# Moving one rotation step, the last outputs and the GELUs in the order of a hybrid layer on one core

## The chip, the core and the metric

The kernel runs on 1 core of one Trainium2 chip. Its time is the device time in microseconds (us) of that core, lower is better.

## The reference

One decoder layer over 256 tokens of width 2048, all in float32:

```python
h = rmsnorm(x)
q, k, v, u = split(h @ w_in, [1024, 1280, 1536])
a = sliding_window_attention(rmsnorm(q), rmsnorm(k), v)   # 16 heads of 64, 4 kv heads, window 128, bias, sinks
s = s5_mixer(u)                                           # 64 groups of 16 channels, 64 complex states
s = gelu(s + d * u); s = s * sigmoid(s @ w_glu)
x = x + concat(rmsnorm(a), rmsnorm(s)) @ w_out
x = x + (silu(rmsnorm(x) @ w_gate) * (rmsnorm(x) @ w_up)) @ w_down
```

## The kernel before

The weights stream from memory in pieces of 512 KB (`w`, 128 partitions x 1024 numbers, four buffers, issued by SyncE). Each piece is split in two: ScalarE's cast makes `whi` (`_piece`, L462) and VectorE's subtraction makes the rest, `wlo` (L463); each has two buffers. A piece feeds 12 matmuls of 128x512 on TensorE (L513 to L515: `whi`, `wlo` and `whi` again, against the high or the low part of the activations). In this order come 16 pieces of `w_u`, 24 of `w_qkv` (the last column block of keys and values first, then the two of queries, of 8 pieces each), 8 of `w_glu`, 32 of `w_out`, and those of the feed-forward part. "Piece 33" below is the 34th from the start.

The S5 mixer runs beside the `w_qkv` pieces, in four parts q=0 to 3 of 16 channel groups. A part has matrices (`m`, two halves, L229), tokens (`u`, L279), a rotation (`r`, L213), states (`s`, L296) and outputs (`o`, L339):

- `rotations` works out cosines `cs` and sines `sn` of a part: VectorE L221 to L223, ScalarE L224 to L226.
- `states` multiplies on TensorE (`px`), transposes into `pa` and `pb` (L310, L315), turns with the rotation on VectorE (`zz` L322, `hh` L323, sum L324), scans (L329) and turns back (L333 to L335).
- `outputs` makes `py` on TensorE (L347, L351); ScalarE copies it to `za` (L353) and issues the DMA write `zd<-za` (L354) to memory.
- `za` and `zz` have the same tag and one buffer between them; so `zz` of one part waits until the write of the part before has read `za`.
- For the matrices, GpSimd issues loads `kd<-kt` (L272) and eight loads `mt<-kd` (L276).

Behind it GpSimd reads `zd` back into `sm` (L692), ScalarE applies the GELU (L695), TensorE transposes into `pt_z` (L697), ScalarE and VectorE split that into `zT` (L698) and `wT` (L699), the operands of the `w_glu` matmuls.

The norms of keys and queries come per token tile (0 and 1), for the keys (4 heads) and then the queries (16 heads): ScalarE squares (`sq`, L713), VectorE sums (`sh`, L715) and scales (L716), GpSimd takes the power -1/2 (`rqk`, L717), VectorE scales the queries' factors (`rqk`, L718) and multiplies the keys (`kvn`, L721). TensorE transposes the keys into `pt_k` (L725). Attention runs in four quads of heads: `pt_q` (L738), `qT` on ScalarE (L739), logits `pl0` and `pl1` on TensorE (L744, L748), `lg` on VectorE (L756) and the exps on ScalarE (L764, L768). The glu has its sigmoids on ScalarE (`sg`, L805 and L808), and L563 there splits what `w_out` multiplies.

What sets the order: each engine's instructions are put in order before the run, by the priority at which a part of the program is traced and by a model of when the inputs are ready; at run time an engine keeps that order and waits. The mixer's steps are all traced at one priority, in the order of the string `STEPS`. `tc.issue_after(mark)` keeps outputs(q) behind the cast of piece `PY_AT[q]`, and the GELU of part q behind that of piece `GELU_AT[q]`:

```python
else:
    with tc.issue_after(marks[PY_AT[q]][1]):
        ssm.outputs(q)
```

Of the kernel before, what the change touches and what calls it, by code (L numbers as in the profile page):

```python
# [39 lines left out]
WORK = dict(tag="t", bufs=4)  # L40


STEPS = "m0a m0b r0 u0 m1a u1 s0 m1b r1 o0 u2 m2a s1 u3 m2b r2 o1 m3a s2 m3b r3 o2 s3 o3"

U_AT = (0, 0, 18, 19)
PY_AT = (14, 19, 25, 32)
GELU_AT = (34, 35, 36, 37)

HEADS = [0, 4, 1, 5, 2, 6, 3, 7, 8, 12, 9, 13, 10, 14, 11, 15]

# [417 lines left out]
def layer_kernel(ctx: ExitStack, tc: tile.TileContext, ins, out):  # L468
# [11 lines left out]
    @contextmanager  # L480
    def prio(at):

        was, tc.cur_priority = tc.cur_priority, at
        try:
            yield
        finally:
            tc.cur_priority = was
# [173 lines left out]
    with prio(20_000):  # L661
        for step in STEPS.split():
            q = int(step[1])
# [8 lines left out]
# [3 lines that stand above are left out]
# [12 lines left out]
    with prio(55_000):  # L687
        for q in range(ngc):
            cols = slice(q * GC * GP, (q + 1) * GC * GP)
            pt = ps.tile([P, 2, L], F32, name="pt_z", **WORK)  # L690
            for t in range(NT):
                nc.gpsimd.dma_start(sm[t][:, cols].rearrange("p (b x) -> p b x", x=UB),  # L692
                                    ssm.zd[4 * q : 4 * q + 4, t * P : (t + 1) * P].rearrange("b p x -> p b x"))
                with tc.issue_after(marks[GELU_AT[q]][0]):
                    s.activation(sm[t][:, cols], sm[t][:, cols], AF.Gelu_apprx_tanh)  # L695
# [268 lines left out]
```

## Time and profile before

| | |
|---|---|
| median of 3 runs | 1066.85 us (1066.33 to 1067.28) |
| profiled execution | 1064.85 us, its span 1063.1 us |
| TensorE (PE) busy | 1043.2 us, 98% |
| VectorE (DVE) busy | 610.9 us, 57% |
| ScalarE (ACT) busy | 485.4 us, 46% |
| GpSimd (POOL) busy | 56.1 us, 5% |

Times in a trace count from the start of the span. An engine is idle either for want of an input, which then has a releaser, or because its order makes it stand behind an instruction that waits. A matmul's row starts when it enters TensorE; the next one may start before it ends, so that the distance between starts counts. `L463` is line 463 of the kernel.

### The profile page before, as it was taken

What the parts mean: (1) busy time and instruction counts of PE and PEld (TensorE: products, weight loads), DVE (VectorE), ACT (ScalarE), POOL (GpSimd) and SP (SyncE); (2) the same over time, 40 slices, a digit from 0 to 9 for tenths busy, and PEclk for the clock granted to TensorE, in tenths of its full rate; (3) what the DMA queues carried; (4) which work ended last, traced back from release to release, by engine and by line L of the source; (5) the groups of instructions that cost most, each with busy time, mean ns of one, the idle gap of its engine ahead of it and who ended that gap; (6) DMA issues with size and microseconds to landing.
All of it is one profiled execution on the core that took longest, in us unless ns stands there. A gap on an engine that the chain in (4) does not pass through costs nothing.

```text
span 1063.1 us, 13209 instructions
## 1 busy us (share of the span) xinstructions
PE 1043.2 (98%) x5048; PEld 820.8 (77%) x5048; DVE 610.9 (57%) x755; ACT 485.4 (46%) x665; POOL 56.1 (5%) x87
## 2 busy tenths in 40 slices
PE   7999988999999999999999999999999999999998
PEld 3457776767788888888888888888888888888886
DVE  6988975788556454445554455545555444444443
ACT  5244556665445444444444444444444333333332
POOL 2030325000000000000000000000000000000000
PEclk9999999999999999999999999999999999999999
DMA  7677567434455556555555555555655556565653
GB/s 268 191 197 237 152 180 267 165 109 139 158 189 167 182 193 189 189 183 194 189 189 195 180 197 185 193 191 184 198 181 196 179 190 207 195 201 195 203 192 101
DMA packets 62015, 199.08 MB, mean 187 GB/s; under 512 B 11328, under 2 KB 14000, under 8 KB 61632
## 3 DMA queue, kind: packets, MB, share of 16 engines
q1 hardware_dynamic: 52800, 184.89, 53.3%
q0 software_dynamic: 3264, 9.29, 3.3%
q10 hardware_dynamic: 5888, 4.06, 1.3%
q8 instruction: 39, 0.64, 0.3%
q14 instruction: 24, 0.20, 0.1%
HBM read 193.47 MB, written 4.74 MB: 186 GB/s over the span
## 4 chain that ended last, share of the span: by engine, by line
PE 85%; DVE 8%; ACT 2%; DMA 2%; issue 2%; POOL 1%; SPq 0%; DVEq 0%; POOLq 0%; ACTq 0%
PE acc L514 26%; PE acc L515 26%; PE acc L513 26%; PE acc L530 2%; DVE wlo L463 1%; PE pt_f L872 1%; DMA zd<-za 1%; POOL rqk L717 1%; PE po L786 1%; DVE bm L249 1%; ACT whi L462 1%; DVE cm L242 1%; DVE bm L250 1%; DVE tm L249 1%; DVE cm L243 1%
## 5 line engine op out<-in xcount | busy, mean ns | idle before, releaser
L463 DVE TENSOR_TENSOR wlo<-w,whi 128x1024 fp32r<-128x1024 f32 x328 | 401.7, 1225 | 407.4 <-ACT whi L462 407.1
L462 ACT CAST whi<-w 128x1024 fp32r<-128x1024 f32 x328 | 345.1, 1052 | 473.1 <-PE acc L515 461.4
L513 PE MATMUL acc<-whi,pTh 128*128 128x512 f32 x704 | 275.0, 391 | 0.0
L514 PE MATMUL acc<-wlo,pTh 128*128 128x512 f32 x704 | 274.0, 389 | 0.2 <-DVE wlo L463 0.2
L515 PE MATMUL acc<-whi,pTl 128*128 128x512 f32 x704 | 274.1, 390 | 0.1
L515 PEld LDWEIGHTS acc<-whi,pTl 128*128 128x128 f32 x704 | 132.1, 188 | 28.0 <-DVE pTl L564 0.5
L514 PEld LDWEIGHTS acc<-wlo,pTh 128*128 128x128 f32 x704 | 132.2, 188 | 27.6 <-DVE wlo L463 0.7
L513 PEld LDWEIGHTS acc<-whi,pTh 128*128 128x128 f32 x704 | 132.2, 188 | 27.6 <-ACT pTh L563 0.5
L513 PE MATMUL acc<-whi,fhi 128*128 128x512 f32 x352 | 139.0, 395 | 0.0
L514 PE MATMUL acc<-wlo,fhi 128*128 128x512 f32 x352 | 138.9, 395 | 0.0
L515 PE MATMUL acc<-whi,flo 128*128 128x512 f32 x352 | 138.9, 394 | 0.0
L515 PEld LDWEIGHTS acc<-whi,flo 128*128 128x128 f32 x352 | 66.3, 188 | 15.5
L513 PEld LDWEIGHTS acc<-whi,fhi 128*128 128x128 f32 x352 | 66.3, 188 | 15.5
L514 PEld LDWEIGHTS acc<-wlo,fhi 128*128 128x128 f32 x352 | 66.3, 188 | 15.3
L513 PE MATMUL acc<-whi,mT 128*128 128x512 f32 x128 | 50.9, 397 | 0.8 <-ACT mT L563 0.8
L514 PE MATMUL acc<-wlo,mT 128*128 128x512 f32 x128 | 50.5, 394 | 0.0
L515 PE MATMUL acc<-whi,nT 128*128 128x512 f32 x128 | 50.3, 394 | 0.0
L514 PE MATMUL acc<-wlo,hT 128*128 128x512 f32 x96 | 38.6, 402 | 2.8 <-DVE wlo L463 2.8
L515 PE MATMUL acc<-whi,lT 128*128 128x512 f32 x96 | 38.0, 396 | 0.0
L513 PE MATMUL acc<-whi,hT 128*128 128x512 f32 x96 | 37.7, 398 | 0.0
L530 PE MATMUL acc<-w,sm 128*128 128x512 f32 x64 | 30.7, 628 | 6.7 <-DVE sm L601 6.7
L884 ACT ACTIVATE sl<-acc,r 128x256 f32<-128x256 f32 x44 | 20.8, 472 | 20.7 <-PE acc L515 20.7
(258 smaller groups left out, 822.0 us busy)
## 6 DMA issues: line engine op xcount, KB each, us to landing
w<-in_w_gu SPq DMA_DIRECT2D x176, 512.0 KB, 3.3
w<-in_w_down SPq DMA_DIRECT2D x88, 512.0 KB, 3.4
w<-in_w_out SPq DMA_DIRECT2D x32, 512.0 KB, 3.3
w<-in_w_qkv SPq DMA_DIRECT2D x24, 512.0 KB, 4.3
w<-in_w_u SPq DMA_DIRECT2D x16, 512.0 KB, 4.0
w<-in_w_glu SPq DMA_DIRECT2D x8, 512.0 KB, 4.3
bias<-td POOLq DMA_DIRECT2D x4, 512.0 KB, 5.1
x<-in_x POOLq DMA_DIRECT2D x2, 1024.0 KB, 10.4
```

Of the source, the lines that this page charges most:

```text
L242: v.tensor_tensor(dst, bc(c[:, i, hs], 2, T), bc(e, 3, GP), op=ALU.mult)
L243: v.tensor_tensor(cmh[:, :, 1:], cmh[:, :, 1:], tm, op=ALU.subtract)
L249: v.tensor_tensor(dst, bc(b[:, i, hs], 2, T), bc(e, 3, GP), op=ALU.mult)
L250: v.tensor_tensor(bm2, bm2, tm2, op=ALU.add)
L462: self.marks.append([nc.scalar.copy(hi, w).ins])
L463: nc.vector.tensor_tensor(lo, w, hi.bitcast(F32), op=ALU.subtract)
L513: mm = pe.matmul(acc[t], lhsT=xh, rhs=whi, start=first, stop=False)
L514: pe.matmul(acc[t], lhsT=xh, rhs=wlo, start=False, stop=False)
L515: pe.matmul(acc[t], lhsT=xl, rhs=whi, start=False, stop=last)
L530: mm = pe.matmul(acc[t], lhsT=x(k)[:, t * P : (t + 1) * P], rhs=w, start=k == 0, stop=k == nk - 1)
L717: nc.gpsimd.tensor_tensor(r_[:, o : o + n], part, cst["mhalf"][:, :n], op=ALU.pow)
L884: s.activation(sl, acc[t][:, :256], AF.Silu, scale=r2[:, t : t + 1])
```

## The change

The rotation of part 3 (`r3`) is traced before the states of part 2 instead of behind `m3b`; the outputs of part 3 are kept behind the cast of piece 29 instead of 32; and each of the four GELUs behind that of one piece earlier. No instruction is added or removed.

```diff
--- before.py
+++ after.py
@@ -40,11 +40,11 @@
 WORK = dict(tag="t", bufs=4)
 
 
-STEPS = "m0a m0b r0 u0 m1a u1 s0 m1b r1 o0 u2 m2a s1 u3 m2b r2 o1 m3a s2 m3b r3 o2 s3 o3"
+STEPS = "m0a m0b r0 u0 m1a u1 s0 m1b r1 o0 u2 m2a s1 u3 m2b r2 o1 m3a r3 s2 m3b o2 s3 o3"
 
 U_AT = (0, 0, 18, 19)
-PY_AT = (14, 19, 25, 32)
-GELU_AT = (34, 35, 36, 37)
+PY_AT = (14, 19, 25, 29)
+GELU_AT = (33, 34, 35, 36)
 
 HEADS = [0, 4, 1, 5, 2, 6, 3, 7, 8, 12, 9, 13, 10, 14, 11, 15]
```

GpSimd's and SyncE's orders stay as they were, and TensorE's does from the second quad's logits on. Elsewhere on TensorE: part 3's output matmuls `py` stood in piece 37 and now stand in piece 38; and 336 weight matmuls of the stretch that starts with `w_qkv` stand before the first quad's `pl0` in place of 324, while 408 stand before the second quad's in both.

**VectorE, the states of part 3.** `hh` and `zz` are those of part 3, `wlo_721` belongs to piece 33 and `wlo_739` to piece 34. Before:

```order
L323 TENSOR_TENSOR hh_1540<-pb_1527,sn_1464 128x512
L463 TENSOR_TENSOR wlo_721<-w_718,whi_720 128x1024
L322 TENSOR_TENSOR zz_1539<-pa_1526,cs_1463 128x512
L327 MEMSET d0_1544 128x16
L324 TENSOR_TENSOR zz_1539<-hh_1540,zz_1539 128x512
L329 SCALAR_TENSOR_TENSOR gg_1547<-d0_1544,zz_1539 128x512
L463 TENSOR_TENSOR wlo_739<-w_736,whi_738 128x1024
```

Now:

```order
L323 TENSOR_TENSOR hh_1540<-pb_1527,sn_1370 128x512
L322 TENSOR_TENSOR zz_1539<-pa_1526,cs_1369 128x512
L463 TENSOR_TENSOR wlo_721<-w_718,whi_720 128x1024
L324 TENSOR_TENSOR zz_1539<-hh_1540,zz_1539 128x512
L329 SCALAR_TENSOR_TENSOR gg_1547<-d0_1544,zz_1539 128x512
L463 TENSOR_TENSOR wlo_739<-w_736,whi_738 128x1024
```

`wlo_721` stood between `hh` and `zz`; now it stands behind both.

**VectorE, the norms of keys and queries.** The digit in `sh0`, `rqk1` and `kvn1` is the token tile; 128x4 is for the keys, 128x16 for the queries. Before:

```order
L716 TENSOR_SCALAR sh0_1651<-sh0_1651 128x16
L716 TENSOR_SCALAR sh1_1665<-sh1_1665 128x4
L463 TENSOR_TENSOR wlo_1774<-w_1771,whi_1773 128x1024
L715 TENSOR_REDUCE sh1_1665<-sq_1672 128x16
L718 TENSOR_SCALAR rqk0_1652<-rqk0_1652 128x16
L721 TENSOR_TENSOR kvn1_78<-kvn1_78,rqk1_1666 128x256
L716 TENSOR_SCALAR sh1_1665<-sh1_1665 128x16
L463 TENSOR_TENSOR wlo_1792<-w_1789,whi_1791 128x1024
L718 TENSOR_SCALAR rqk1_1666<-rqk1_1666 128x16
```

Now:

```order
L716 TENSOR_SCALAR sh0_1651<-sh0_1651 128x16
L715 TENSOR_REDUCE sh1_1665<-sq_1667 128x4
L715 TENSOR_REDUCE sh1_1665<-sq_1672 128x16
L463 TENSOR_TENSOR wlo_1792<-w_1789,whi_1791 128x1024
L716 TENSOR_SCALAR sh1_1665<-sh1_1665 128x4
L716 TENSOR_SCALAR sh1_1665<-sh1_1665 128x16
L718 TENSOR_SCALAR rqk0_1652<-rqk0_1652 128x16
L718 TENSOR_SCALAR rqk1_1666<-rqk1_1666 128x16
L721 TENSOR_TENSOR kvn1_78<-kvn1_78,rqk1_1666 128x256
L463 TENSOR_TENSOR wlo_1916<-w_1913,whi_1915 128x1024
```

`kvn1` (L721) stood ahead of `rqk1` (L718) and now stands behind it, and one weight subtract is gone from between the norm's steps (it stands further ahead now). ScalarE's squares are now all behind part 3's two GELUs, of which one square stood ahead.

**ScalarE, where the first quad's exps begin** (`sg` is the glu's, `es` and `lg,dn` are exps of the first quad's logits, `whi` is a weight piece's cast). Before:

```order
L805 ACTIVATE sg<-acc_1733 128x512
L764 ACT_TABLE_LOAD
L764 ACTIVATE es<-es 128x8
L462 CAST whi<-w 128x1024
L808 ACTIVATE sg,sss<-sm_79 128x512
L768 ACTIVATE lg,dn<-lg,mx 128x128
L462 CAST whi<-w 128x1024
```

Now:

```order
L805 ACTIVATE sg<-acc_1733 128x512
L462 CAST whi<-w 128x1024
L808 ACTIVATE sg,sss<-sm_79 128x512
L764 ACT_TABLE_LOAD
L764 ACTIVATE es<-es 128x8
L462 CAST whi<-w 128x1024
L805 ACTIVATE sg<-acc_1734 128x512
L768 ACTIVATE lg,dn<-lg,mx 128x128 x2
L462 CAST whi<-w 128x1024
```

The table load and `es` stood ahead of the first L808 and now stand behind it. From that L808 to the second quad's `qT` there are eight exps, three L805, three further L808 and four L563 in both orders, but five casts where there were four.

## Rows read from the trace of the kernel before

**Rows 1.** The page's first part, and windows: window, TensorE's length and busy time first.

```profile
PE 1043.2 (98%) x5048; PEld 820.8 (77%) x5048; DVE 610.9 (57%) x755; ACT 485.4 (46%) x665; POOL 56.1 (5%) x87
...
185.10:216.00 30.90, 28.89 (x126) 21.05 (x126) 23.99 (x46) 20.61 (x45) 3.29 (x3) 1.00 0.53 176
216.00:330.00 114.00, 113.85 (x554) 87.47 (x554) 78.68 (x124) 66.42 (x143) 1.51 (x2) 1.00 0.44 143
```

**Rows 2.** Waits of TensorE in 140 to 216: total us, times, longest.

```profile
PE acc L514 <- DVE wlo L463: 2.9, 3, 2.2
PE pt_k L725 <- DVE kvn L721: 1.4, 1, 1.4
```

**Rows 3.** The chain in 138 to 216: start us, us, what.

```profile
141.96 6.12 DMA zd<-za
...
163.70 3.17 DMA zd<-za
...
168.14 3.93 DMA sm<-zd
```

**Rows 4.** Timeline of VectorE (DVE) around 146: start us, us, instruction, idle time before.

```profile
144.60 0.69 DVE L323 TENSOR_TENSOR hh<-pb,sn 128x512 f32<-128x512 f32 x1 [4.05 <-PE pb L315]
...
148.10 0.69 DVE L322 TENSOR_TENSOR zz<-pa,cs 128x512 f32<-128x512 f32 x1 [1.68 <-DMA zd<-za]
```

**Rows 5.** DMA issues in 78 to 82, then in 114 to 118: KB, us to landing.

```profile
zd<-za ACTq DMA_DIRECT2D x1, 256.0 KB, 7.8
...
zd<-za ACTq DMA_DIRECT2D x1, 256.0 KB, 4.8
```

**Rows 6.** Timeline of GpSimd (POOL), 115 to 187.

```profile
115.24 3.40 POOL L276 DMA_DIRECT2D mt<-kd  x7
...
138.35 3.86 POOL L276 DMA_DIRECT2D mt<-kd  x8 [3.15 <-PE acc L515]
...
172.89 1.04 POOL L717 TENSOR_TENSOR rqk<-sh,mhalf 128x4 f32<-128x4 f32 x1 [1.08 <-DVE sh L716]
...
178.52 3.92 POOL L717 TENSOR_TENSOR rqk<-sh,mhalf 128x16 f32<-128x16 f32 x2 [3.49 <-DVE sh L716]
183.06 3.81 POOL L717 TENSOR_TENSOR rqk<-sh,mhalf 128x16 f32<-128x16 f32 x1 [0.62 <-DVE sh L716]
```

**Rows 7.** Timeline of TensorE (PE), 154 to 211.

```profile
154.60 0.39 PE L513 MATMUL acc<-whi,hT 128*128 128x512 f32 x1
...
157.35 0.39 PE L513 MATMUL acc<-whi,hT 128*128 128x512 f32 x1
...
161.06 0.42 PE L347 MATMUL py<-mt,ua 128*32 128x128 f32 x8
...
182.95 0.55 PE L725 MATMUL pt_k<-pack,kvn 128*128 128x128 f32 x3 [1.37 <-DVE kvn L721]
...
210.65 1.02 PE L744 MATMUL pl<-kT,qT 128*128 128x256 f32 x4
```

**Rows 8.** Timeline of VectorE in 178 to 187.

```profile
178.63 1.23 DVE L463 TENSOR_TENSOR wlo<-w,whi 128x1024 fp32r<-128x1024 f32 x1
...
182.47 0.42 DVE L721 TENSOR_TENSOR kvn<-kvn,rqk 128x256 f32<-128x256 f32 x1 [0.81 <-POOL rqk L717]
...
182.89 1.22 DVE L463 TENSOR_TENSOR wlo<-w,whi 128x1024 fp32r<-128x1024 f32 x1
186.90 0.17 DVE L718 TENSOR_SCALAR rqk<-rqk 128x16 f32<-128x16 f32 x1 [2.79 <-POOL rqk L717]
```

**Rows 9.** Timeline of ScalarE (ACT), 194 to 210.

```profile
194.57 1.28 ACT L764 ACT_TABLE_LOAD   x1
...
195.98 1.03 ACT L462 CAST whi<-w 128x1024 fp32r<-128x1024 f32 x1
196.92 0.63 ACT L808 ACTIVATE sg<-sm 128x512 f32<-128x512 f32 x1
...
209.70 0.67 ACT L739 ACTIVATE qT<-pt_q,pack 128x512 f32<-128x512 f32 x1
```

## The prediction, before the changed kernel was run

> **What bounds the kernel now.** The page's first line gives TensorE 1043.2 us busy, 98% of the span [rows 1], so the kernel is a stream of matmuls and only TensorE's idle time can be won or lost. The windows say where that idle time lies: 0.15 us in 216 to 330, but 2.01 us in 185.1 to 216 alone [rows 1], and more ahead of it. The change reorders work before 216 alone (behind the second attention quad's first `pl0` the TensorE order is the same), so what counts is how late TensorE arrives there: 210.65 now [rows 7]. The waits view names what it waits for in this stretch: `wlo` from VectorE (2.9 us in all, once 2.2) and `pt_k` for `kvn` (1.4) first [rows 2]. The chain view goes one step further back. The 2.2 us wait ends a chain that comes through the DMA write `zd<-za` of 6.12 us; another, which ends in the GELUs and the `pt_z` transposes of q=3, goes through a write of 3.17 us and the read back `sm<-zd` of 3.93 us [rows 3]. The write is in VectorE's way because `zz` (L322) reuses the buffer `za` that the write reads: `zz` starts at 148.10, 1.68 us idle, released by that DMA [rows 4]. Everything counts against the profiled execution's 1064.85 us, 2.00 below the median of the runs; I add my difference to the median, 1066.85.
>
> **Part 1, the last states step.** No instruction is added or removed; 12 matmuls of a weight piece take 157.35 - 154.60 = 2.75 us [rows 7] on either side. Now `pa` and `pb` of q=3's states come earlier relative to what they need, which saves some 0.4 us: an estimate, from `hh` waiting until 144.60 for `pb` [rows 4]. In exchange the VectorE order puts both `hh` and `zz` ahead of the weight subtract `wlo_721`, where before only `hh` was. That subtract (1.23 us by another of its kind, [rows 8]) now waits for the write of q=2's output. I put its issue at 142.05, as before within 0.1 (the chain shows 141.96). How long it takes is not known. The four writes of this kernel took 3.2 to 7.8 us: 7.8 and 4.8 the first two [rows 5], 6.1 and 3.2 the last two [rows 3]. The 6.1 us write started behind all eight `mt` loads of its step (issued 138.35 to 142.21); the 4.8 us one at 115.69 went beside them (115.24 on) [rows 5, 6]. In the new order the `mt` loads are issued about 3 us later, alongside, which is nearest to 4.8. So the write lands at 146.85; `zz` at 146.9 takes 0.69; `wlo_721` runs 147.5 to 148.7, and TensorE waits some 2.1 us in that piece. The wait of 2.2 us one piece later then shrinks to about 0.4, as its subtract `wlo_739`, behind the same `zz` either way, ends 0.2 us sooner at about 151.7. Net at the next piece (154.60 before, [rows 7]): **-0.2 us**. One wait is swapped for another.
>
> **Part 2, the last outputs.** The diff queues them three pieces sooner, yet the TensorE order shows q=3's `py` one piece later (with its inputs due earlier, other work went ahead of it). Hence its start moves from 161.06 [rows 7] by 2.75 - 0.2 = 2.55 to 163.6, and with the same write, read back and GELU behind it (3.17 and 3.93 us, [rows 3]) the last GELU goes from 172.1 (168.14 + 3.93) to about 174.65.
>
> **Part 3, the k/q norm.** It is traced behind that GELU and now also runs behind it: ScalarE does both GELUs of q=3 before the first square, which was in front. GpSimd's 128x16 `pow` of token tile 0 started at 178.52 [rows 6], 6.4 us behind the last GELU. In the new order ScalarE has a cast and a copy `qn` less in between and a square more (-1.3, an estimate), VectorE one weight subtract more (+0.85, the part of its 1.23 that isn't beside ScalarE's work). So it starts 5.95 behind 174.65, at 180.6. On VectorE the new order then has `L718 rqk1` in front of `L721 kvn1`, which was the other way round. L718 needs the last 128x16 `pow`; TensorE's `pt_k` needs L721. Before, L721 waited only for the 128x4 `pow` (0.81 us, [rows 8]), and the last `pow`, 183.06 to 186.87, was beside the path, holding L718 at 186.90 [rows 6, 8]. Now it is on the path. What is one 128x16 `pow`? The pair of 3.92 us is one of 128x16 and one of 128x4; the latter alone took 1.04 us at 172.89 [rows 6], so 2.9. The single one took 3.81. The 2.9 one began before a weight subtract, the 3.81 one inside one (182.89 to 184.11, [rows 8]). In the new order none runs when the last `pow` starts, as VectorE stands at L718; I take 2.9, with 3.81 as bound (+0.9). Then: 180.6 + 2.9 + 1.04 = 184.55, + 2.9 = 187.45 for the last `pow`, about 0.6 us for L718, L721 and the hand-over (0.48 for the latter two, 182.47 to 182.95, [rows 7, 8]): `pt_k` at 188.1, where it was 182.95 [rows 7], 5.15 us later. TensorE has by then done 12 matmuls more (its order puts them ahead), 2.75 us. So the delay is **+2.4 us**, the -0.2 of part 1 included; the wait at `pt_k` grows from 1.4 to about 3.5 us.
>
> The Trainium skill's page "SBUF — State Buffer", section "Who interferes with whom", has a rule that speaks against the subtracts near these `pow`s: a VectorE instruction with two SBUF inputs and a GpSimd instruction that reads SBUF exclude each other, and the one that starts second waits for all of the first. The 3.81 us row agrees (it began 0.17 us into a subtract and took 0.9 more), but the other speaks against it: the subtract at 178.63, 0.11 us into a `pow`, took 1.23 us as ever [rows 8]. By the rule the time would be that of rival 4, by that row the forecast stands.
>
> **Part 4, ScalarE before the second quad.** Here the first quad's exps, the glu work and the casts fill ScalarE: 20.61 of 30.9 us in 185.1 to 216 [rows 1]. `qT` (L739) is ready at 209.70 + 0.67 and the second `pl0` follows at 210.65 [rows 7, 9], so ScalarE's order sets it. Between the first L808, at 196.92, and `qT` the new order has one cast more (1.03 us), and the exps' table load with `es` (194.57 to 195.98, 1.4 us), which stood ahead of that L808 [rows 9]: together 2.4 us. L808 itself I put 1.8 later rather than 2.4, since the table load is no longer ahead of it. So `qT` and the second `pl0` are 1.8 + 2.4 = 4.2 later, which is **+1.8** on top of the 2.4. TensorE, with 72 matmuls between the two `pl0` where 84 were, then waits about 2.5 to 3 us there. Of the 2.01 us idle some 0.4 lies behind it, in waits for the logits, and shrinks (an estimate): **-0.4 us**. Nothing else changes after 216, and no slack is left there to take it back (0.15 us, [rows 1]). The moved GELU at each earlier q costs nothing: its due time moves by one piece, and its input is there long before.
>
> **The sum**: 2.4 + 1.8 - 0.4 = **+3.8 us**, so 1068.65 for the profiled execution and 1066.85 + 3.8 = 1070.65, **1070.6**, for the median. Bounds: the write at 3.2 us gives -1.6, at 6.1 +1.3, at 7.8 +3.0; the `pow` at 3.81 gives +0.9. The forecast's own range is about 1069.1 to 1072.
>
> **Rivals.**
> 1. Not slower: ScalarE absorbs it. TensorE idles 2.01 us between 185.1 and 216 [rows 1]. If the table load and the added cast are through before TensorE gets to the second `pl0`, at 210.65 + 2.4 - 2.0 = 211.0, then most of the +2.4 is eaten there and +0.4 remains: 1067.3. It decides at one point, whether `qT` ends before 211. For it: ScalarE has 10.3 us idle in that window. Against: `qT` starts at 209.70 [rows 9], with the glu's L808 right ahead of it, and the reordering adds to that queue. Chance 0.16; with an early write also, 1065.7.
> 2. The write lands early (3.2 us, as the last one did): 3.8 - 1.6 = +2.2, so 1069.0. For it: one of four was that fast. Against: that one had no `mt` loads beside it, as GpSimd's order has none left by then. Chance 0.13.
> 3. The write lands late (6.1 to 7.8 us): +5.1 to +6.8, so 1072.0 to 1073.6. For it: the write just there took 6.1. Chance 0.11.
> 4. A subtract is held by the first long `pow` until it ends: the second token tile's inputs come about 1.5 us later, and so `pt_k`: 1072.2. Chance 0.05, by the row against it.
>
> **How the numbers follow.** The forecast has 0.55. A difference of 0.2%, 2.1 us, is about what a measurement can tell from none. Faster by more than that needs rival 1 and luck in the write: 0.04. Within it lie the rest of rival 1 (0.14), half of rival 2 (0.07) and the forecast's low edge (0.04): 0.25. The rest, 0.71, is slower. The range, from rival 1's 1067.3 less a little, to rival 3's upper end, is 1067.0 to 1073.7.
>
> **What would show it.** Right: a wait of about 2 us before the first `wlo` matmul in the piece of `wlo_721`, behind `zz` and the DMA `zd<-za`; q=3's `py` near 163.6; a wait of 3 to 4 us at `pt_k` for `kvn`, with L718 and GpSimd's last `pow` just ahead; a wait of 2 to 3 us at the second `pl0` for `qT`; TensorE as full as before after 220. Wrong: `pt_k` at or before 186, or `qT` ready before TensorE asks, or `wlo_721` not held by `zz`.

## The result and the profile after

| | before | changed |
|---|---|---|
| median of 4 runs | 1067.07 us (1066.33 to 1067.46) | 1072.73 us (1071.96 to 1075.28) |
| profiled execution | 1064.85 us, span 1063.1 | 1073.29 us, span 1071.5 |
| TensorE's mean granted clock in that span | 0.999 | 0.996 |

The changed kernel is slower: ratio 1.0059, 95% interval 1.0047 to 1.0072, 5.7 us by the medians. It lies inside the predicted range (1067.0 to 1073.7), 2.1 us above the predicted time.

The page's first line of the changed kernel, which answers to [rows 1]: TensorE's share is 98% as before, yet its busy time grew by 5.1 us although it does the same 5048 instructions.

```profile
PE 1048.3 (98%) x5048; PEld 822.4 (77%) x5048; DVE 611.5 (57%) x755; ACT 484.9 (45%) x665; POOL 55.1 (5%) x87
```

The waits view of TensorE, changed kernel, 140 to 232 (total us, times, longest), which answers to [rows 2]:

```profile
PE pt_k L725 <- DVE kvn L721: 3.8, 2, 3.3
PE pl L744 <- ACT qT L739: 2.9, 1, 2.9
PE acc L514 <- DVE wlo L463: 2.2, 3, 1.4
PE pt_z L697 <- ACT sm L695: 1.4, 1, 1.4
```

The wait for `wlo` is smaller than before (2.2 in all after 2.9), that for `pt_k` has grown from 1.4 to a longest of 3.3, and a wait of 2.9 for `qT` at the second quad's `pl0` is new. That is what was forecast, at the places that were forecast. What was not forecast is in the windows of the same stretch (window, its length, busy time and instructions of PE, PEld, DVE, ACT and POOL, then TensorE's granted clock, the DMA share and GB/s):

```profile
184.70:188.20 3.50, 0.16 (x2) 0.01 (x1) 0.57 (x3) 0.00 (x0) 2.90 (x2) 1.00 0.98 397
...
189.40:191.00 1.60, 1.60 (x5) 1.31 (x5) 0.00 (x0) 0.80 (x2) 0.00 (x0) 0.50 0.52 90
...
197.00:213.70 16.70, 16.06 (x73) 12.16 (x72) 12.18 (x20) 14.65 (x35) 0.05 (x2) 1.00 0.59 190
213.70:216.60 2.90, 0.05 (x1) 0.00 (x0) 1.68 (x4) 2.86 (x8) 0.70 (x1) 0.94 0.60 181
216.60:218.50 1.90, 1.89 (x5) 1.53 (x6) 1.83 (x2) 0.00 (x0) 0.00 (x0) 0.50 0.64 213
...
226.00:337.00 111.00, 110.87 (x538) 85.55 (x535) 75.60 (x117) 65.11 (x140) 0.72 (x1) 1.00 0.45 142
```

TensorE hardly works from 184.7 to 188.2, and from 213.7 to 216.6. About the end of each, its granted clock falls to 0.50, which is 1.2 GHz in place of 2.4 (the second time just ahead of 216.6, hence the 0.94); before that, in between and from 226 on it is 1.00. The four matmuls of the first `pl0` show it in their duration: 1.77 us (at 190.84, in the rows below), where the same row of the kernel before took 1.10:

```profile
185.08 1.10 PE L744 MATMUL pl<-kT,qT 128*128 128x256 f32 x4 [0.18 <-issue]
```

The rows that answer to [rows 4] and [rows 8], VectorE's timeline in the changed kernel; first `zz` and the subtract behind it:

```profile
147.07 0.69 DVE L322 TENSOR_TENSOR zz<-pa,cs 128x512 f32<-128x512 f32 x1 [3.62 <-DMA zd<-za]
147.68 1.21 DVE L463 TENSOR_TENSOR wlo<-w,whi 128x1024 fp32r<-128x1024 f32 x1
```

then the norm, with the subtract that runs beside a `pow`:

```profile
182.12 1.21 DVE L463 TENSOR_TENSOR wlo<-w,whi 128x1024 fp32r<-128x1024 f32 x1
...
187.63 0.18 DVE L718 TENSOR_SCALAR rqk<-rqk 128x16 f32<-128x16 f32 x1 [3.68 <-POOL rqk L717]
187.72 0.42 DVE L721 TENSOR_TENSOR kvn<-kvn,rqk 128x256 f32<-128x256 f32 x1
```

`zz` waits 3.62 us for the write and `wlo_721` starts behind it, at 147.68. At 187.63 VectorE has stood 3.68 us at L718 for GpSimd's last `pow`, and only then, at 187.72, come the keys that TensorE wants. The chain view between 180 and 190 has the `pow`s themselves (start, us), as [rows 6] had them:

```profile
180.82 2.76 POOL rqk L717
...
183.73 3.88 POOL rqk L717 x2
```

TensorE's timeline at the places of [rows 7]:

```profile
163.77 0.43 PE L347 MATMUL py<-mt,ua 128*32 128x128 f32 x8
...
188.19 0.55 PE L725 MATMUL pt_k<-pack,kvn 128*128 128x128 f32 x3 [3.34 <-DVE kvn L721]
...
190.84 1.77 PE L744 MATMUL pl<-kT,qT 128*128 128x256 f32 x4
...
216.62 2.08 PE L744 MATMUL pl<-kT,qT 128*128 128x256 f32 x4 [2.86 <-ACT qT L739]
```

and ScalarE's, as [rows 9]:

```profile
200.52 0.63 ACT L808 ACTIVATE sg<-sm 128x512 f32<-128x512 f32 x1 [1.95 <-DVE mx L760]
...
201.26 1.28 ACT L764 ACT_TABLE_LOAD   x1
...
215.90 0.67 ACT L739 ACTIVATE qT<-pt_q,pack 128x512 f32<-128x512 f32 x1
```

The table load now stands behind an L808 which itself waited 1.95 us, and `qT` starts at 215.90 where it started at 209.70.

### The profile page after: what moved, and what is told of

It reads as the page before. It is cut to its first block, busy times and chain, and to the rows that moved or that the text cites. A ratio compares the mean times of both kernels' runs of the same rounds, so it can differ in the third digit from the quotient of the medians.

```text
span 1071.5 us, 13211 instructions
## 1 busy us (share of the span) xinstructions
PE 1048.3 (98%) x5048; PEld 822.4 (77%) x5048; DVE 611.5 (57%) x755; ACT 484.9 (45%) x665; POOL 55.1 (5%) x87
## 4 chain that ended last, share of the span: by engine, by line
PE 89%; DVE 3%; ACT 2%; DMA 2%; issue 2%; POOL 1%; SPq 0%; DVEq 0%; POOLq 0%; ACTq 0%
PE acc L514 26%; PE acc L515 26%; PE acc L513 26%; PE acc L530 5%; DVE wlo L463 1%; PE pt_f L872 1%; ACT whi L462 1%; POOL rqk L717 1%; PE pl L748 1%; DMA zd<-za 1%; PE po L786 1%; PE pl L744 1%; PE pp L780 0%; DMA w<-in_w_u 0%; PE pt_bm L264 0%
```

## The experiments

Each ratio is to the kernel before, run on the same chip, with its 95% interval; it is not the quotient of the two medians and can differ a little from it. Experiments 1, 2 and 8 to 11 start from the kernel before, the others from the changed kernel.

**1. The steps alone.**

```diff
-STEPS = "... m3a s2 m3b r3 o2 s3 o3"
+STEPS = "... m3a r3 s2 m3b o2 s3 o3"
```

> Only the string of steps is changed; the due times of the outputs and the GELUs stay as before. Theory: the whole loss is in the steps, so 1071.5 to 1073.5 us, with the waits of the changed kernel at pt_k (about 3.3 us) and at the second pl0 (about 2.9 us) and TensorE's granted clock at 0.5 behind each. Rival (the due times cost it): within 1 us of the kernel before, 1066 to 1068.

Measured: 1074.84 us, ratio 1.0085 (1.0070 to 1.0100). The waits of the changed kernel are there (3.32 at `pt_k`, 2.89 at the second `pl0`), and the clock of 0.50 behind both. The time is 1.3 us above the expected span, on another chip, with mean clocks of 0.993 to 0.996. So the string of steps carries the whole loss. The due time of the last outputs does nothing by itself: taken back in the changed kernel, or put alone into the kernel before, it leaves the order of all five engines as it was, row for row.

**2. The GELUs' due times alone.**

```diff
-GELU_AT = (34, 35, 36, 37)
+GELU_AT = (33, 34, 35, 36)
```

> Only the due times of the GELUs are changed (the due time of the last outputs changes no engine's order, so this is the order of both due times together). Theory: the due times are not what costs, 1065.5 to 1068.5 us, no wait over 2.5 us at pt_k or at the second pl0. Rival (the due times cost it): 1070 or more.

Measured: 1066.93 us, ratio 1.0013 (0.9999 to 1.0027). Its longest waits are 1.65 for `wlo` and 1.61 for `pt_z`. By the interval the due times cost 0.27% at most, so they are not what costs the 0.59%.

**3. The keys ahead of the last `pow`.**

```diff
-            v.tensor_scalar_mul(r_[:, :NH], r_[:, :NH], HD**-0.5)
             rq.append(r_)
             kk = kvn[t][:, : NKV * HD].rearrange("p (h d) -> p h d", d=HD)
             v.tensor_tensor(kk, kk, bc(r_[:, NH:], 2, HD), op=ALU.mult)
+            v.tensor_scalar_mul(r_[:, :NH], r_[:, :NH], HD**-0.5)
```

> The changed kernel, with the scaling of the queries' factors traced behind the scaling of the keys, so that L721's work of token tile 1 no longer stands behind the last pow; ScalarE's order is the same. Theory: pt_k waits 0.6 to 1.0 us in place of 3.3, TensorE's granted clock stays at 1.00 behind it, and the time falls by 2.5 to 4.5 us from the changed kernel, to 1068.3 to 1070.3. Rival (what sets the later time is ScalarE's order alone): the wait moves to the second pl0 and the time falls by less than 1 us, 1071.7 to 1072.7.

Measured: 1073.47 us, ratio 1.0073 (1.0058 to 1.0088), nothing won. Both theories missed it. The waits of TensorE (140 to 232), and VectorE's timeline:

```profile
PE acc L514 <- DVE wlo L463: 4.6, 4, 2.3
PE pl L744 <- ACT qT L739: 2.9, 1, 2.9
PE pt_k L725 <- DVE kvn L720: 1.1, 2, 0.6
```

```profile
184.56 0.44 DVE L720 TENSOR_TENSOR kvn<-kvn,rqk 128x256 f32<-128x256 f32 x1 [0.82 <-POOL rqk L717]
187.43 0.17 DVE L721 TENSOR_SCALAR rqk<-rqk 128x16 f32<-128x16 f32 x1 [2.43 <-POOL rqk L717]
187.52 1.22 DVE L463 TENSOR_TENSOR wlo<-w,whi 128x1024 fp32r<-128x1024 f32 x1
```

The keys are ready at 184.56 and `pt_k` waits only 0.6 us. But VectorE then stands 2.43 us at the scaling of the queries' factors (L721 in this kernel), and the weight subtract behind it, at 187.52, comes nearly as late as before (188.05): the wait has moved from `pt_k` to `wlo` (2.3 us). So the error in my account of part 3 was to look at the keys alone. **What costs is that VectorE itself stands there**; all that is queued behind it is late. TensorE's clock fell to 0.50 after this pair of shorter waits too.

**4. A buffer of its own for `za`.**

```diff
-        z = self.sp.tile([P, T, 4, GP], F32, name="za", tag="zz")
+        z = self.sp.tile([P, T, 4, GP], F32, name="za", tag="za")
```

> The changed kernel, with za in a buffer of its own, so that zz no longer waits for the write of the part before. Theory: the waits for wlo in pieces 33 and 34 (1.4 and 0.2 us) go and all behind them comes 1.5 to 2 us sooner, 1070.7 to 1071.3. Rival (that stretch is absorbed by later waits): the pt_z and pt_k waits grow by what was won and the time stays within 0.5 us of 1072.7.

Measured: 1072.79 us, ratio 1.0072 (1.0055 to 1.0089). In its profile the wait in piece 33 is 0.2 in place of 1.4, and the wait at `pt_z` grew from 1.4 to 1.8. `pt_k` starts 0.57 us sooner than in the changed kernel, or 0.9 when the later start of this execution is taken off (120.27 against 119.97 at the same matmul). The second `pl0`, at 214.88, starts 1.74 sooner, but 1.2 of this is the clock, as told below. The time is the rival's; in the profile 0.4 of the 1.2 us that the wait lost went into the wait at `pt_z`, and 0.9 was won, which the runs are too scattered to show. Their scatter is what this kernel taught: 1070.03 us at a mean clock of 0.999, and 1071.86, 1073.72 and 1074.14 at 0.997, 0.994 and 0.995. The profiled execution is the first of these. Its windows, in the same columns:

```profile
184.20:187.60 3.40, 0.11 (x1) 0.00 (x0) 0.54 (x3) 0.00 (x0) 2.83 (x1) 1.00 0.85 347
...
189.00:191.00 2.00, 1.98 (x8) 1.30 (x8) 0.12 (x1) 0.64 (x1) 0.00 (x0) 1.00 0.63 184
...
211.80:214.80 3.00, 0.18 (x1) 0.00 (x0) 1.71 (x5) 3.00 (x9) 0.71 (x1) 1.00 0.54 176
214.80:216.50 1.70, 1.62 (x6) 1.25 (x7) 1.67 (x3) 0.03 (x1) 0.00 (x0) 1.00 0.56 140
```

TensorE idles here as it does in the changed kernel, 3.3 us at `pt_k` and 2.9 at the second `pl0`, and in this execution its clock stays at 1.00 behind both:

```profile
187.62 0.55 PE L725 MATMUL pt_k<-pack,kvn 128*128 128x128 f32 x3 [3.30 <-DVE kvn L721]
...
214.88 1.13 PE L744 MATMUL pl<-kT,qT 128*128 128x256 f32 x4 [2.90 <-ACT qT L739]
```

From `pt_k` to the second `pl0` the orders of the two kernels are the same, and so is all that follows; the stretch takes 27.26 us here (187.62 to 214.88) and 28.43 in the changed kernel (188.19 to 216.62): the first fall of the clock cost 1.2 us. From the second `pl0` to the next weight matmul behind the logits of the next quad it is 12.87 us (to 227.75) and 14.33 (to 230.95): the second cost 1.5. **2.6 us together**. The price comes from this one execution without the falls, against one with them; that they are paid in most executions the mean clocks show. Of the 16 runs of the changed kernel and experiments 1, 3 and 4, 15 are at 0.997 or less. Of the 77 runs of the kernel before that were made beside the experiments, 58 are at 0.999 or more; the other 19 are 1.7 to 3.3 us longer, by the medians on each chip, so the kernel before has a fall in some executions too, though its profiled one has none.

The page "TensorE: Matmul & The Clock Gate" of the Trainium skill, section "What's actually happening", says that the clock follows how busy the engine has been, and that the point at which it changes varies from run to run. The two profiles agree: the same idle time, once with a clock of 0.50 behind it and once without.

**5. L718 folded away.**

```diff
-                v.tensor_scalar(part, part, 1.0 / HD, EPS, op0=ALU.mult, op1=ALU.add)
+                v.tensor_scalar(part, part, (1.0 if n == NH else 1.0 / HD), (HD * EPS if n == NH else EPS), op0=ALU.mult, op1=ALU.add)
...
-            v.tensor_scalar_mul(r_[:, :NH], r_[:, :NH], HD**-0.5)
```

The factor 1/8 of the queries is 64 inside the power -1/2.

> The changed kernel without the two instructions of L718: their factor is folded into the constants of L716, so that nothing on VectorE waits for the last pow before the logits. The orders are otherwise the changed kernel's. Theory (what costs is VectorE standing at L718, wherever L721 stands): pt_k waits 0.6 to 1.0 us, the wlo wait of the run with the keys first does not come back, the granted clock stays at 1.00 up to 210, the first quad's pl0 starts 3 to 4 us sooner than in the changed kernel; the wait at the second pl0 for qT stays at 2.5 to 3.2 us. 1067.5 to 1069.5 us. Rival (ScalarE's order alone sets the second pl0): the wait there grows by what was won, 1071.5 or more.

Measured: 1069.49 us, ratio 1.0028 (1.0015 to 1.0042), so 0.31% less than the changed kernel's ratio, some 3.3 us; the two intervals don't overlap. The waits and two windows:

```profile
PE pl L744 <- ACT qT L739: 2.9, 1, 2.9
PE acc L514 <- DVE wlo L463: 2.5, 2, 2.0
...
PE pt_k L725 <- DVE kvn L721: 0.4, 1, 0.4
```

```profile
190.00:192.00 2.00, 1.88 (x7) 1.32 (x8) 0.74 (x3) 0.03 (x1) 0.35 (x1) 1.00 0.87 277
...
215.40:217.40 2.00, 1.92 (x5) 1.56 (x6) 1.86 (x3) 0.03 (x1) 0.00 (x0) 0.50 0.62 213
```

The wait at `pt_k` is 0.4, the wait for `wlo` that is left near it is 0.5, and the clock is 1.00 at the first `pl0` (190 to 192). The wait of 2.9 for `qT` and the half clock behind that (215.4 on) are left. But the clock did not stay at 1.00 up to there, as was expected. In this execution it fell twice before, once behind the wait of 2.0 for `wlo` that ended at 149.61 and once behind one of 1.75 for `pt_z` that ended at 177.39; the two windows that hold these falls have a mean clock of 0.79 and 0.94:

```profile
146.00:154.00 8.00, 5.98 (x20) 4.44 (x19) 6.14 (x8) 4.12 (x8) 1.57 (x2) 0.79 0.61 146
154.00:184.00 30.00, 28.25 (x183) 22.89 (x183) 16.06 (x21) 16.37 (x25) 7.67 (x10) 0.94 0.66 214
```

With that its first `pl0`, at 190.12, is 0.7 us sooner than in the changed kernel and not 3 to 4, and the execution (1071.23) is 1.7 above the median. The times tell the two accounts of experiment 3 apart: moving the keys ahead of the standing instruction won nothing, removing that instruction won it.

**6. `qT` early.**

```diff
-        s.activation(qT, pt, AF.Copy, scale=cst["qkg"][:, 0:1])
+        with prio(64_000):
+            s.activation(qT, pt, AF.Copy, scale=cst["qkg"][:, 0:1])
```

> The changed kernel with qT traced at a higher priority, so that ScalarE makes it ahead of the casts, exps and glu work; the second quad's pl0 then stands 34 matmuls earlier on TensorE. The first wait (pt_k) stays. Theory: the 2.9 us wait at the second pl0 and the half clock behind it go, 1068 to 1070 us. Rival (other work late for the same reason takes its place, as exps or casts come later): a new wait of 2 us or more on TensorE before 230, 1071 or more.

Measured: 1070.40 us, 0.4 above the expected span, ratio 1.0038 (1.0024 to 1.0051), 0.21% under the changed kernel's ratio, though the two intervals just overlap; the trace tells it more clearly:

```profile
PE pt_k L725 <- DVE kvn L721: 3.8, 2, 3.3
...
PE pp L781 <- DVE rs_a L492: 0.7, 1, 0.7
```

The wait for `qT` is gone, with one of 0.7 in its place further on; the 3.3 at `pt_k` is left, as it should be.

**7. Both.**

> Both of the last two edits in the changed kernel. Theory (the two waits and the clock behind them are the whole loss): at the kernel before or up to 2 us under it, 1064 to 1067 us, granted clock 0.999 or more. Rival (the new order loses elsewhere too): 1068 or more.

Measured: 1067.66 us, ratio 1.0010 (0.9996 to 1.0023), which can't be told from the kernel before. 0.49% is won where the two alone won 0.31% and 0.21%: they add, within these intervals.

```profile
PE acc L514 <- DVE wlo L463: 2.4, 2, 1.9
PE pt_z L697 <- ACT sm L695: 1.1, 1, 1.1
PE pt_k L725 <- DVE kvn L721: 1.1, 2, 0.6
PE pp L781 <- DVE rs_a L492: 0.7, 1, 0.7
```

The median is 0.7 us above the span that was expected, and seven of the ten runs miss the expected clock of 0.999. In the profiled one it fell behind the wait of 1.9 for `wlo` that is left (0.83 on average in 146 to 154). So the two waits and the clock behind them are the greater part of the loss; that they are all of it is not shown, as the interval holds a rest of 0.23% as well as none.

**8. The kernel before without L718** (the edit of 5).

> The kernel before without L718. Its order there had L721 ahead of the last pow; VectorE stood 2.8 us at L718 for the last pow, and TensorE waited about 1 us for the subtract behind it. Theory: that wait goes and the logits start sooner, 0.5 to 1.5 us less than the kernel before. Rival (ScalarE, filled from 194 to 210, sets the second pl0): within 0.3 us of it.

Measured: 1066.51 us, ratio 0.9995 (0.9982 to 1.0007). The wait for `wlo` at 188.56 (0.4 us in the waits view, not the 1 us that was expected) is gone in the profile, and the time doesn't show it. Inconclusive between the gain that was forecast and none.

**9 to 11. The kernel before with the other edits**: the buffer of 4; that and the edit of 5; both and the edit of 6.

> The kernel before with za in a buffer of its own. Theory: its wait of 2.2 us for wlo in piece 34 goes, and all behind comes 1.5 to 2.2 us sooner: ratio to the kernel before 0.998 to 0.9985. Rival (the waits at pt_z and pt_k grow by it, as part of it did in the changed kernel): within 0.5 us of the kernel before.

Measured: 1065.59 us, ratio 0.9995 (0.9982 to 1.0007). The wait of 2.2 us shrinks to 0.5 in the profile; what was won in the time is not told from none.

> The kernel before with that buffer and without L718. Theory: both gains add, 2 to 3 us under the kernel before. Rival (absorbed ahead of the second pl0): the same as the kernel before within 0.7 us.

Measured: 1064.75 us against 1066.95 on this chip, ratio 0.9986 (0.9974 to 0.9998). This is the fastest of all, 2.2 us by the medians and 1.5 by the ratio, at the edge of what can be told. Sorted by clock, which was done after the result, the runs say more. Those at a mean clock of 0.999 or more have these medians: 1066.28 us in experiment 8 (8 runs), where the kernel before has 1066.36 (22 runs); 1065.12 in experiment 9 (7 runs) and 1064.47 here (8 runs), where it has 1066.53 (25 runs). So in executions at full clock the buffer wins some 1.4 us, L718 alone nothing that is seen, and both 2.1.

> The kernel before with the buffer, without L718 and with qT early. Theory: 2.5 to 4.5 us under the kernel before, the fastest of all. Rival (the order that follows from an early qT loses as much as the 0.9 us wait for mT that it removes): like the run without the early qT.

Measured: 1067.25 us, ratio 1.0001 (0.9987 to 1.0015). The early `qT` gives all of it back, 0.15% by the ratios, though the two intervals overlap. Its order lets another wait grow:

```profile
PE pt_k L725 <- DVE kvn L721: 2.8, 1, 2.8
```

which was 1.4 before. Behind it the clock fell to 0.50 in the profiled execution, and ten of the eleven runs have a mean clock under 0.999. Neither theory nor rival held: the rival had put the time at that of the run without the early `qT`.

**12. The changed kernel with all three edits.**

> The changed kernel with the buffer, without L718 and with qT early: all three waits that were found are taken out. Theory (nothing but these waits and the clock behind them was lost by the change): 1 to 3 us under the kernel before, within 1.5 us of the kernel before with the same three edits. Rival (the later outputs of part 3 cost the piece by which they are later): 2.5 us or more above that one.

Measured: 1066.47 us, ratio 0.9992 (0.9981 to 1.0002), 0.8 us under the kernel before with the same edits. It is 0.5 us under the kernel before, where 1 to 3 were expected. The waits left between 140 and 232 are these:

```profile
PE pt_z L697 <- ACT sm L695: 2.4, 2, 2.1
PE acc L514 <- DVE wlo L463: 1.0, 3, 0.5
PE pp L781 <- DVE rs_a L492: 0.7, 1, 0.7
```

With its waits taken out the changed order of steps can't be told from the old one. The wait of 2.1 at `pt_z` was followed by a fall of the clock in this execution (0.94 on average in 154 to 184). How much of it is due to the later outputs is not shown.

## Why the prediction was right, and where its size was off

The direction, the places and the waits were right, the size was 2 us short. By its own steps, on the two profiled executions; TensorE is 0.68 us later in the changed one already at 120 (119.97 against 119.29 at the same matmul), ahead of all that the change moves, and this is taken off:

- **Part 1**, -0.2 forecast: the next piece starts at 154.56 where it did at 154.60, so -0.7 without the 0.68. `wlo_721` was held by `zz` as forecast, and TensorE waited 1.4 us for it, 2.1 forecast. The write took 4.2 us where 4.8 was taken from its neighbour in kind.
- **Part 2**: `py` at 163.77, 163.6 forecast (164.3 with the 0.68). It is later by one piece, as the order showed, against what the diff says.
- **Part 3**, +2.4 forecast: `pt_k` at 188.19, 188.1 forecast. Less 2.75 for the 12 matmuls and 0.68 this is 5.24 - 3.43 = +1.8. The last `pow` took 3.88 - 1.04 = 2.8 us, so of the two prices the one without a subtract at its start was the right choice. The wait was 3.3, 3.5 forecast. But experiments 3 and 5 correct the reason: L718 ahead of L721 is not the point, L718 ahead of everything on VectorE is.
- **The rule from the Trainium skill's page "SBUF — State Buffer", section "Who interferes with whom", rival 4**: the subtract at 182.12 ran 1.21 us, its usual time, with a `pow` under way since 180.82. It was not held, and the rival did not come. The row that spoke against the rule was the better guide: here the measurement decides. The row that agreed with it came again: in experiments 8, 9 and 10 a `pow` that began 0.17 us into a subtract took 3.81 us as well, where those that began clear of one took 2.8 to 2.9.
- **Part 4**, +1.8 forecast: the second `pl0` comes at 216.62, 5.97 later, so 5.3 without the 0.68, 4.2 forecast. 1.2 of it is the clock behind the first wait (experiment 4), so the queue on ScalarE was priced right at 4.1. Experiment 6 shows that this queue was the cause.
- **The later waits**, -0.4 forecast, and "TensorE as full as before after 220": up to the weight matmul at 230.95 (223.63 before) the kernel is 7.32 later, 6.6 without the 0.68. Here 1.5 more of clock came in, and the waits shrank by 0.1 alone.

So without the clock the stretch cost 6.6 - 2.6 = 4.0 us, and the sum said 3.8. **The step that failed is a term that the sum did not have**: it priced a wait of TensorE at its own length. In the trace of before the longest wait, 2.2 us, was followed by a clock of 1.00, so no row warned of it; the two forecast waits of 3.5 and 2.5 to 3 us were longer than any wait there, and that should have been a bound upwards. From 230 to the end another 1.1 us comes in while TensorE is full in both and no wait is to be seen. Of this 1.0 lies in the last thousand matmuls, which take 232.1 us in the trace of before and 233.1 in that of the changed kernel. It goes with the execution and not with the change: in experiment 8, whose TensorE order is that of the kernel before, they take 233.1 too, and in experiment 5, whose order there is that of the changed kernel, 232.1. What slows them is open.

So of the 8.4 us between the two profiled executions, 1.7 has nothing to do with the change. The medians differ by 5.7, 1.9 more than the sum; the clock's 2.6, less what it takes from some executions of the kernel before, would cover that, but no run splits the medians.

That the time lies in the range owes something to luck. At 1072.7 it is above the forecast's own range (1069.1 to 1072) and inside the wide one by the bound of rival 3, whose late write did not happen. And in the chances the rest of rival 1 is 0.16 - 0.04 = 0.12, where 0.14 was put.

Rival 1 (absorbed by ScalarE) failed at the point it named: `qT` had not ended by 211 but started at 215.90. Rivals 2 and 3 were not needed: the write's 4.2 us lies between their 3.2 and 6.1, near the 4.8 taken.

## What to carry to other kernels

An instruction that waits for a slow engine costs by what is queued behind it on its own engine, not only by who reads its result: moving the reader ahead of it won nothing, taking the instruction away won 0.3%. Read the order that a change really gives on each engine, since a due time may move nothing and an earlier step in the trace may end later. And price a new wait of two or three us on TensorE at its length plus the slower matmuls that may follow it, as a bound upwards.

## What the runs showed of the hardware

TensorE's granted clock can fall to 0.50 behind a wait that interrupts a full stretch. In the profiles here it fell behind waits of 2.9 to 3.3 us (the changed kernel), of 2.8 (experiment 11), 2.1 (experiment 12), 2.0 and 1.75 (experiment 5) and 1.9 (experiment 7), and with the keys first (experiment 3) behind one of 0.6 and one of 2.3 close together. It stayed at 1.00 behind waits of 3.3 and 2.9 in experiment 4, 2.2 in the kernel before and 2.0 in experiment 8. So the length of a wait alone did not settle it. The two falls in the changed kernel cost 1.2 and 1.5 us. A GpSimd `pow` of 128x16 takes 2.8 to 2.9 us and one of 128x4 1.0; one of 128x16 that began 0.17 us into a VectorE subtract took 3.8, while a subtract that starts inside a `pow` was not slowed.
